# An MLP's second token half, prepared in pieces between six opening pairs on VectorE

## The chip, the cores and the metric

The kernel runs on one core of a Trainium2 chip. A core has a matrix engine (TensorE, PE in the profile), three engines for elementwise work (VectorE or DVE, ScalarE or ACT, GpSimd or POOL), a queue that issues transfers (SyncE or SP), an on-chip memory of 128 partitions that the kernel divides into tiles, and an accumulator memory (PSUM) into which TensorE writes. The metric is the time of one execution in device microseconds; lower is better.

## The reference

A small encoder of two layers over 1024 tokens of width 1024. Layer 0 mixes tokens with windowed attention beside a pooling mixer, layer 1 with latent attention beside a recurrent block. Each layer ends with the same kind of MLP, and this is what the change touches:

```python
def rmsnorm(x, g):
    y = x * lax.rsqrt(jnp.mean(x * x, axis=-1, keepdims=True) + EPS)
    return y * g

def sq_relu_mlp(h, w1, w2):
    u = jax.nn.relu(h @ w1)        # 1024 x 1024 times 1024 x 4096
    return (u * u) @ w2            # 1024 x 4096 times 4096 x 1024

for layer in range(2):
    x = x + mixer(layer, rmsnorm(x, norm[layer]))
    x = x + sq_relu_mlp(rmsnorm(x, norm_mlp[layer]), w_mlp1[layer], w_mlp2[layer])
return rmsnorm(x, final_norm)
```

All of it is in 32-bit floats.

## The kernel before

**Layout.** The activations stand transposed: channels on the partitions, tokens along the free axis. X is eight tiles of 128 channels by 1024 tokens. A token half is 512 columns; `lo` and `hi` in the norm of the MLP are the first and the second half.

**Split operands.** TensorE gets each 32-bit operand as two parts, high and low: ScalarE rounds the value to the matrix format (the high part, `rnd`, line 122, or line 278 with a sign), VectorE subtracts to get the low part (`sub`, line 130, or line 279). Each 128-deep step is three matmuls: high by high, low by high, high by low. `block()` (line 272) makes such a pair for a 128x512 operand; blocks of activations are named `hb`, blocks of weights `wb`.

**Strassen-like products.** An MLP's first matrix product works on 2x2 blocks: two token halves, two channel halves, two weight chunks (a pair p out of 16). Seven products serve for eight. For the weights the seven operands are A11, A12, A22 and sums S1 to S4, which POOL adds; for the activations they are B11 and B21 (the first token half's two channel halves) and t2, t3, T1, t4, B22, each of four channel chunks, which need the second token half also. One product (line 367) is 4 chunks times 3 matmuls, 12 matmuls of 128x512.

**Order in an MLP (`mlp`, line 348).** NS = 4 pairs open the MLP. For these, only the two products that need the first token half are done first: `head` (A11 by B11, copied to t1) and `head2` (A12 by B21, then relu and square to u11). After them `rest` does the five other products of each of these pairs, with their weights loaded again, and then pairs 4 to 15 run with all seven products. The results u11, u12, u21, u22 and their sums go to DRAM (`put`, line 378). The second matrix product (`second`, line 470) reads them back, in three groups of pairs, and adds into X, which `load_x` (line 247) reads back from DRAM before it begins. The last two pairs (TAIL) are plain products.

**Weights as a stream.** `w_stream` yields one weight block after the other in a given order, and `Ahead` keeps three more than the one that is taken (W_AHEAD = 3). So the instructions that make a block stand in the program four products ahead of its use. A block sits in one of eight weight tiles (W_BUFS); four of the eight hold two prefetched weights of TAIL all through an MLP.

**The norm of the MLP (`SNorm`, line 1453).** `part(c, cut)` is called by the output projection before the MLP when channel chunk c of a token half is final. It squares the chunk on ScalarE and adds it to `acc` on POOL (`square_add`, line 238); in the second half it writes X to DRAM (line 1472). `sums` (a matmul with ones, line 220, and the root) and `finish` (the factor broadcast by matmul, line 231, and copied to RB) follow. `finish(0)` scales all eight chunks of the first half into new tiles H (line 1492) and makes B11 and B21. `finish(1)`, which is called after the second head, does the whole second half: it scales eight chunks, subtracts (lines 1507 and 1509, VectorE), subtracts and adds on POOL (lines 1512 and 1516), and makes the 20 blocks t2, t3, T1, t4, B22.

**The projection before it.** In the even layer `outproj_halves` (line 730) does eight output chunks for the first token half, then eight for the second, and loads each of its four weights for both halves. In the odd layer, the loop at line 1143 does the same with eight weights.

**Buffers.** Most tiles of 128x1024 come from one pool with 41 buffers (G_BUFS). U and H2 hand out halves of such a tile.

**What sets the order.** The program is traced in Python; a planner then orders the instructions of each engine, with the traced order as their priority, by a simulated timeline, and adds the waits. On the chip each engine and each queue runs its list in that order.

The wait for a tile of the pool is one of these waits, and so a transfer into a tile that isn't free yet holds up what stands behind it in the queue.

Of the kernel before, what the change touches and what calls it, by code (L numbers as in the profile page):

```python
# [15 lines left out]
P = 128  # L16
# [30 lines left out]
class Trunk:  # L47
# [89 lines left out]
    def requests(self, ph):  # L137
        a = self.a
        if ph == "even":
            r = [(a["e_w_in"][i], S) for i in (4, 5, 0, 1, 2, 3)] + [(a["e_w_pool"], N2)]  # L140
            r += [(a["e_w_in"][i], S) for i in (9, 8, 7, 6)]
            r += [(a["e_w_out"][1][m], S, "act", "pool") for m in range(4)]
            return r + [(a["e_w_out"][0][m], S) for m in range(4)] * 2
# [203 lines left out]

    def mlp(self, l, nb, nxt, dram):
# [4 lines left out]
        main = ("A11", "S2", "S3", "S1", "A12", "A22", "S4")  # L353
        start = range(NS)
        order = [x for p in start for x in [(p, "A11")] + [(p - 1, "A12")] * (p > 0)] + [(NS - 1, "A12")]
        order += [(NP + p, b) for p in start for b in ("S2", "S3", "S1", "A22", "S4")]
        order += [(p, b) for p in range(NS, NP) for b in main]
        stream = Ahead(self.w_stream(l, order, False), W_AHEAD)
# [71 lines left out]
        for p in start:  # L430
            ps = self.PS("q")
            early[p] = (*head(p, ps), ps)
            if p == 0:
                nb.sums(1)
            if p == 1:
                nb.finish(1)
            if p:
                head2(p - 1, early[p - 1][2], early[p - 1][1])
        head2(NS - 1, early[NS - 1][2], early[NS - 1][1])
        k = 0  # L440
# [24 lines left out]
        X = self.load_x(nb.spill)  # L465
# [13 lines left out]

        for g, pairs in enumerate(GROUPS):  # L480
# [7 lines left out]
            B = self.banks(1 - k)  # L488
            second(B, pairs, True, False)
            for m in range(4):  # L490
                V.tensor_tensor(X[4 + m][:, h1], B[m], X[4 + m][:, h1], op=ALU.add)  # L491
            second(A, pairs, False, True)
# [237 lines left out]
    def outproj_halves(self, X, Yh, Yl, done):  # L730

        for n in range(2):
            s = slice(n * N2, (n + 1) * N2)
            for mm in range(NC // 2):
                W = self.weight()
                for j in range(2):
                    m = 2 * mm + j
                    ps = self.PS("op")
                    self.mm3(ps, [(W[0][:, (j * 4 + k) * P:(j * 4 + k + 1) * P],
                                   W[1][:, (j * 4 + k) * P:(j * 4 + k + 1) * P], Yh[k][:, s], Yl[k][:, s])  # L740
                                  for k in range(4)])
                    self.nc.vector.tensor_tensor(X[m][:, s], ps, X[m][:, s], op=ALU.add)
                    done(m, HALVES[n])
# [709 lines left out]
class SNorm:  # L1453

    cuts = [(0, N2), (N2, S)]

    def __init__(self, t, X, gname, spill):
        self.t, self.X, self.g, self.spill = t, X, gname, spill  # L1460
        self.acc, self.r, self.T = {}, {}, {}
        self.RB = t.G("RB")
        self.H = None

    def part(self, c, cut):
        t = self.t
        n = HALVES.index(cut)
        if c == 0:
            self.acc[n] = t.tp.tile([P, N2], F32, tag="acc", name=t.nm("acc"), bufs=2)
        t.square_add(self.acc[n], self.X[c][:, slice(*cut)], c == 0)  # L1470
        if n == 1:
            t.nc.sync.dma_start(self.spill[c * P:(c + 1) * P, :], self.X[c])
            if c == 2:
                self.sums(0)
            if c == 4:
                self.finish(0)
# [4 lines left out]
    def finish(self, n):  # L1481
        t, nc = self.t, self.t.nc
        V = nc.vector
        s = slice(n * N2, (n + 1) * N2)
        lo, hi = slice(0, N2), slice(N2, S)
        t.rb_bcast(self.r[n], self.RB[:, s])
        if n == 0:
            self.H = [t.G("H") for _ in range(NC)]
        H = self.H

        def scaled(c):
            V.scalar_tensor_tensor(H[c][:, s], self.X[c][:, s], t.col(self.g, c), self.RB[:, s],
                                   op0=ALU.mult, op1=ALU.mult)

        def blocks(name, xs, neg=False):
            self.T[name] = [t.block("hb", x, neg=neg) for x in xs]

        if n == 0:
            for name, r in (("B11", range(4)), ("B21", range(4, 8))):
                for c in r:  # L1500
                    scaled(c)
                blocks(name, [H[c][:, s] for c in r])
            return
        t2 = [t.U("t2") for _ in range(4)]
        for c in range(4):
            scaled(c)
# [12 lines left out]


class Ahead:
# [5 lines left out]
    def take(self):  # L1527
        while len(self.have) <= self.ahead:
# [3 lines left out]
            self.have.append(x)  # L1532
        return self.have.pop(0)
# [88 lines left out]
NS = 4  # L1622
# [16 lines left out]
def trunk(tc, a, phases=("even", "mlp0", "odd", "mlp1", "final")):  # L1639
    PSUM = bass.MemoryType.PSUM  # L1640
    with tc.tile_pool(name="cst", bufs=1) as cst, tc.tile_pool(name="sm", bufs=4) as sm, \
# [11 lines left out]
        def follow(i):  # L1653

            def make(X):
# [3 lines left out]
                    SNorm(t, X, gains[ph], xm[int(ph[-1])])  # L1659
# [104 lines left out]
```

## Time and profile before

| | us |
|---|---|
| median of 3 runs | 2253.13 (2248.68 to 2254.84) |
| the profiled execution | 2256.08 |
| its span | 2254.2 |
| TensorE busy in it | 2067.0 |
| VectorE busy | 1539.7 |
| ScalarE busy | 1063.9 |
| GpSimd busy | 865.4 |
| matmuls of the first MLP products, L367 (2688) | 643.7 |
| matmuls of the second MLP products, L477 (2352) | 540.4 |

The profile has one page for an execution, and views that can be asked for: the same stretch of time by engine (windows), groups of instructions by line, the waits, and the timeline. Busy time of TensorE includes pipelining: at full rate, matmuls of 128x512 start every 0.225 us though each shows as about 0.39 us. "Idle before, releaser" names what ended an engine's wait. The granted clock is the share of full speed that TensorE was given.

MLP 0 begins at about 313 us and MLP 1 at about 1542 us in the profiled execution. Their second stages begin at 701.6 and 1916.5 us.

### The profile page before, as it was taken

What the parts mean: (1) busy time and instruction counts of PE and PEld (TensorE: products, weight loads), DVE (VectorE), ACT (ScalarE), POOL (GpSimd) and SP (SyncE); (2) the same over time, 40 slices, a digit from 0 to 9 for tenths busy, and PEclk for the clock granted to TensorE, in tenths of its full rate; (3) what the DMA queues carried; (4) which work ended last, traced back from release to release, by engine and by line L of the source; (5) the groups of instructions that cost most, each with busy time, mean ns of one, the idle gap of its engine ahead of it and who ended that gap; (6) DMA issues with size and microseconds to landing.
All of it is one profiled execution on the core that took longest, in us unless ns stands there. A gap on an engine that the chain in (4) does not pass through costs nothing. (4 is left out here: it accounts for less than half of the span.)

```text
span 2254.2 us, 27294 instructions
## 1 busy us (share of the span) xinstructions
PE 2067.0 (92%) x9600; PEld 1695.6 (75%) x9600; DVE 1539.7 (68%) x2345; ACT 1063.9 (47%) x1857; POOL 865.4 (38%) x659
## 2 busy tenths in 40 slices
PE   7989984999998999999997999896799998999997
PEld 5867763777776788888775998785577776788887
DVE  7788756655555877764897888617665564877874
ACT  5247543444444444331565777634444444444423
POOL 4143244322224241332557675464322221513314
PEclk9999986999999999999999999998899999999999
DMA  5630041444357536122102000233253445554412
GB/s 168 159 113 20 22 157 61 164 145 149 108 171 290 185 102 195 66 80 89 33 33 56 10 15 6 94 126 126 104 180 119 149 146 212 197 193 133 148 37 75
DMA packets 113240, 261.32 MB, mean 116 GB/s; under 512 B 19408, under 2 KB 21584, under 8 KB 113104
## 3 DMA queue, kind: packets, MB, share of 16 engines
q1 hardware_dynamic: 113104, 259.59, 34.5%
q8 instruction: 75, 1.23, 0.2%
q14 instruction: 61, 0.50, 0.1%
HBM read 178.28 MB, written 72.35 MB: 111 GB/s over the span
## 5 line engine op out<-in xcount | busy, mean ns | idle before, releaser
L367 PE MATMUL q<-hb,wb 128*128 128x512 f32 x2688 | 643.7, 399 | 104.4 <-ACT wb L122 76.0
L367 PEld LDWEIGHTS q<-hb,wb 128*128 128x128 f32 x2688 | 511.0, 192 | 235.5 <-ACT wb L122 88.1
L477 PE MATMUL q<-ub,wb 128*128 128x512 f32 x2352 | 540.4, 392 | 15.5 <-ACT ub L122 10.5
L477 PEld LDWEIGHTS q<-ub,wb 128*128 128x128 f32 x2352 | 443.8, 189 | 112.2 <-ACT ub L122 11.3
L130 DVE TENSOR_TENSOR wb<-raw,wb 128x512 fp32r<-128x512 f32 x268 | 226.0, 850 | 130.5 <-ACT wb L122 129.8
L122 ACT CAST wb<-raw 128x512 fp32r<-128x512 f32 x268 | 163.3, 618 | 201.2 <-PE q L367 107.8
L327 POOL TENSOR_TENSOR sum<-raw 128x512 f32<-128x512 f32 x32 | 41.7, 1302 | 404.8 <-DMA raw<-in_w_dram 306.6
L130 DVE TENSOR_TENSOR ub<-ut,ub 128x512 fp32r<-128x512 f32 x168 | 136.2, 821 | 57.9 <-ACT ub L122 57.8
L122 ACT CAST ub<-ut 128x512 fp32r<-128x512 f32 x168 | 101.5, 619 | 149.7 <-DMA ut<-ut_12t 19.0
L130 DVE TENSOR_TENSOR wb<-sum,wb 128x512 fp32r<-128x512 f32 x152 | 128.3, 846 | 58.0 <-ACT wb L122 57.4
L245 POOL TENSOR_TENSOR acc<-acc,sq 128x512 f32<-128x512 f32 (+1 forms) x70 | 101.9, 1458 | 138.2 <-ACT sq L244 136.5
L122 ACT CAST wb<-sum 128x512 fp32r<-128x512 f32 x152 | 93.5, 618 | 120.7 <-PE q L367 50.8
L185 PE MATMUL z<-Hh,wh 128*128 128x512 f32 x336 | 132.6, 398 | 9.6 <-ACT wh L122 9.6
L185 PE MATMUL z<-Hl,wh 128*128 128x512 f32 x336 | 133.2, 397 | 4.0 <-DVE Hl L1439 3.8
L185 PE MATMUL z<-Hh,wl 128*128 128x512 f32 x336 | 132.0, 394 | 0.0
L323 POOL TENSOR_TENSOR sum<-raw,raw 128x512 f32<-128x512 f32 x28 | 40.1, 1435 | 221.7 <-DMA raw<-in_w_dram 156.0
L122 ACT CAST wh<-raw 128x1024 fp32r<-128x1024 f32 (+1 forms) x53 | 54.0, 1018 | 114.3 <-PE z L185 38.9
L1092 PE MATMUL cav<-cpT,VS 128*128 128x256 f32 x512 | 102.2, 303 | 5.4 <-ACT cpT L1321 2.8
L1302 PE MATMUL ms<-Kt,Qt 128*128 128x512 f32 (+1 forms) x384 | 100.5, 398 | 2.3 <-ACT e L1309 1.4
L1322 DVE TENSOR_TENSOR cpT<-ctp,cpT 128x512 fp32r<-128x512 f32 x128 | 86.6, 686 | 16.6 <-ACT cpT L1321 13.9
L185 PE MATMUL op<-yh,wh 128*128 128x512 f32 x244 | 96.6, 397 | 1.2 <-DVE ya L855 0.6
L1074 POOL TENSOR_SCALAR e<-e,csm 128x1024 f32<-128x1024 f32 x64 | 71.9, 1126 | 64.6 <-DVE csm L1073 51.4
(349 smaller groups left out, 3874.3 us busy)
## 6 DMA issues: line engine op xcount, KB each, us to landing
raw<-in_w_dram SPq DMA_DIRECT2D x136, 512.0 KB, 4.6
xm<-X SPq DMA_DIRECT2D x16, 512.0 KB, 3.0
X<-xm SPq DMA_DIRECT2D x16, 512.0 KB, 5.6
raw<-in_o_w_out_dram SPq DMA_DIRECT2D x16, 512.0 KB, 3.4
raw<-in_e_w_out_dram SPq DMA_DIRECT2D x12, 512.0 KB, 3.5
raw<-in_o_w_in_dram SPq DMA_DIRECT2D x11, 512.0 KB, 3.4
raw<-in_e_w_in_dram SPq DMA_DIRECT2D x10, 512.0 KB, 4.4
X<-in_x_dram SPq DMA_DIRECT2D x16, 256.0 KB, 5.4
```

Of the source, the lines that this page charges most:

```text
L122: self.nc.scalar.copy(out, x)
L130: e.tensor_tensor(out, x, y, op=ALU.subtract)
L185: self.nc.tensor.matmul(ps, l, r, start=(first and i == 0), stop=(last and i == n - 1))
L245: (eng or nc.gpsimd).tensor_tensor(acc, acc, sq, op=ALU.add)
L323: add(x, blk(p, 1, 0), blk(p, 1, 1), op=ALU.add)
L327: add(s1, blk(p, 1, 0), blk(p, 1, 1), op=ALU.add)
L367: nc.tensor.matmul(ps, a, b, start=(first and c == 0 and i == 0), stop=(c == 3 and i == 2), skip_group_check=True)
L477: nc.tensor.matmul(ps[m], a, b, start=(first and j == 0 and i == 0), stop=(j == len(pairs) - 1 and i == 2), skip_group_check=True)
L1074: nc.gpsimd.tensor_scalar(e, e, sm, 1.0, op0=ALU.mult, op1=ALU.mult)
L1092: nc.tensor.matmul(ACC[0][:, (p % 2) * 256:(p % 2 + 1) * 256], VS[h][:, kb * P:(kb + 1) * P], pp[:, t * N2 + ii * 256:t * N2 + (ii + 1) * ...
L1302: nc.tensor.matmul(ps[:, s], l[rows, qs], r[rows, s], start=(i == 0), stop=(i == 2))
L1322: nc.vector.tensor_tensor(pp[:, N2:], tp, pp[:, :N2], op=ALU.subtract)
```

## The change

- `NS` goes from 4 to 6: six pairs open an MLP instead of four.
- `SNorm` makes the weight stream itself when it is created. In the second half of the projection, `part` calls `sums(0)` at chunk 1, the factor at chunk 2, makes the first four weight blocks (`fill`) at chunk 4, and from chunk 3 on scales the first half and makes B11 and B21, a few chunks at each call.
- X is scaled in place; there are no tiles H. X is written to DRAM by token halves, as each is final.
- From chunk 4 of the second half on, the sum of squares is added on VectorE instead of POOL.
- `finish(1)` becomes the generator `late`, in ten pieces. Two pieces are traced per opening pair, one before and one after `head2`. Its subtractions and additions are all on VectorE.
- `mlp` reads X back later: chunks 4 to 7 ahead of the second product group's use of them, chunks 0 to 3 after it.
- `outproj_halves` keeps its four weights for both halves, and loads each once.

```diff
-            return r + [(a["e_w_out"][0][m], S) for m in range(4)] * 2
+            return r + [(a["e_w_out"][0][m], S) for m in range(4)]
...
             early[p] = (*head(p, ps), ps)
             if p == 0:
                 nb.sums(1)
-            if p == 1:
-                nb.finish(1)
-            if p:
+                late = nb.late()
+            else:
+                next(late)
                 head2(p - 1, early[p - 1][2], early[p - 1][1])
+                next(late)
         head2(NS - 1, early[NS - 1][2], early[NS - 1][1])
+        for _ in late:
+            pass
...
-        X = self.load_x(nb.spill)
+        X = [self.G("X") for _ in range(NC)]
...
+        def load(ms):
+            for m in ms:
+                dma(X[m], nb.spill[m * P:(m + 1) * P, :])
...
             B = self.banks(1 - k)
+            if g == 0:
+                load(range(4, 8))
             second(B, pairs, True, False)
...
+            if g == 0:
+                load(range(4))
             second(A, pairs, False, True)
...
             for mm in range(NC // 2):
-                W = self.weight()
+                if n == 0:
+                    ws.append(self.weight())
+                W = ws[mm]
...
+        self.stream = t.first_stream(l)
...
-        t.square_add(self.acc[n], self.X[c][:, slice(*cut)], c == 0)
-        if n == 1:
-            t.nc.sync.dma_start(self.spill[c * P:(c + 1) * P, :], self.X[c])
-            if c == 2:
-                self.sums(0)
-            if c == 4:
-                self.finish(0)
+        t.square_add(self.acc[n], self.X[c][:, s], c == 0, t.nc.vector if n and c > 3 else None)
+        t.nc.sync.dma_start(self.spill[c * P:(c + 1) * P, s], self.X[c][:, s])
+        if n == 0:
+            return
+        if c == 1:
+            self.sums(0)
+        elif c == 2:
+            self.factor(0)
+        elif c >= 3:
+            if c == 4:
+                self.stream.fill()
+            for k in ((0, 1), (2, 3), (4,), (5,), (6, 7))[c - 3]:
+                self.scaled(k, 0)
+                self.T["B11" if k < 4 else "B21"].append(t.block("hb", self.X[k][:, :N2]))
...
+    def scaled(self, c, n):
+        s = slice(n * N2, (n + 1) * N2)
+        x = self.X[c][:, s]
+        self.t.nc.vector.scalar_tensor_tensor(x, x, self.t.col(self.g, c), self.RB[:, s], op0=ALU.mult, op1=ALU.mult)
+
+    def late(self):
+        t, H, T = self.t, self.X, self.T
+        V = t.nc.vector
         lo, hi = slice(0, N2), slice(N2, S)
+        for name in ("t2", "t3", "T1", "t4", "B22"):
+            T[name] = []
+        self.factor(1)
+        t2 = []
         for c in range(4):
-            scaled(c)
+            self.scaled(c, 1)
             V.tensor_tensor(H[c][:, lo], H[c][:, hi], H[c][:, lo], op=ALU.subtract)
-            scaled(4 + c)
+            self.scaled(4 + c, 1)
+            t2.append(t.U("t2"))
             V.tensor_tensor(t2[c], H[c][:, lo], H[4 + c][:, hi], op=ALU.subtract)
-        blocks("t2", t2)
+            T["t2"].append(t.block("hb", t2[c]))
+            yield
         for c in range(4):
-            nc.gpsimd.tensor_tensor(H[c][:, hi], H[c][:, hi], H[4 + c][:, hi], op=ALU.subtract)
-        blocks("t3", [H[c][:, hi] for c in range(4)])
-        blocks("T1", [H[c][:, lo] for c in range(4)])
+            V.tensor_tensor(H[c][:, hi], H[c][:, hi], H[4 + c][:, hi], op=ALU.subtract)
+            T["t3"].append(t.block("hb", H[c][:, hi]))
+            if c % 2:
+                yield
         for c in range(4):
-            nc.gpsimd.tensor_tensor(H[4 + c][:, lo], H[4 + c][:, lo], t2[c], op=ALU.add)
-        blocks("t4", [H[4 + c][:, lo] for c in range(4)])
-        blocks("B22", [H[4 + c][:, hi] for c in range(4)], neg=True)
+            T["T1"].append(t.block("hb", H[c][:, lo]))
+        yield
+        for c in range(4):
+            V.tensor_tensor(H[4 + c][:, lo], H[4 + c][:, lo], t2[c], op=ALU.add)
+            T["t4"].append(t.block("hb", H[4 + c][:, lo]))
+            if c % 2:
+                yield
+        for c in range(4):
+            T["B22"].append(t.block("hb", H[4 + c][:, hi], neg=True))
+        yield
...
-NS = 4
+NS = 6
```

`first_stream` gives the order of the weight blocks that `mlp` gave itself before: A11 of pair 0, then A11 of pair p and A12 of pair p - 1 in turn, A12 of the last opening pair, the five blocks of each rest pair, and the seven of each other pair.

More of the change, by code (lines that the diff above doesn't have):

```diff
@@ L346, in w_stream, with first_stream @@
             yield prep(p, b)
+    def first_stream(self, l):
+        start = range(NS)
+        order = [x for p in start for x in [(p, "A11")] + [(p - 1, "A12")] * (p > 0)] + [(NS - 1, "A12")]
+        order += [(NF // 2 + p, b) for p in start for b in ("S2", "S3", "S1", "A22", "S4")]
+        order += [(p, b) for p in range(NS, NF // 2) for b in ("A11", "S2", "S3", "S1", "A12", "A22", "S4")]
+        return Ahead(self.w_stream(l, order, False), W_AHEAD)
     def mlp(self, l, nb, nxt, dram):
@@ L352, in mlp @@
         NP = NF // 2
-        main = ("A11", "S2", "S3", "S1", "A12", "A22", "S4")
         start = range(NS)
[L355 to L358, printed above, removed]
+        stream = nb.stream
         def product(ps, blocks, first, last):
@@ L730, in outproj_halves @@
     def outproj_halves(self, X, Yh, Yl, done):
+        ws = []
         for n in range(2):
@@ L1457, with __init__ @@
     cuts = [(0, N2), (N2, S)]
-    def __init__(self, t, X, gname, spill):
+    def __init__(self, t, X, gname, spill, l):
         self.t, self.X, self.g, self.spill = t, X, gname, spill
-        self.acc, self.r, self.T = {}, {}, {}
+        self.acc, self.r, self.T = {}, {}, {"B11": [], "B21": []}
         self.RB = t.G("RB")
-        self.H = None
+        self.stream = t.first_stream(l)
     def part(self, c, cut):
@@ L1467, in part @@
         n = HALVES.index(cut)
+        s = slice(*cut)
         if c == 0:
             self.acc[n] = t.tp.tile([P, N2], F32, tag="acc", name=t.nm("acc"), bufs=2)
-        t.square_add(self.acc[n], self.X[c][:, slice(*cut)], c == 0)
-        if n == 1:
-            t.nc.sync.dma_start(self.spill[c * P:(c + 1) * P, :], self.X[c])
-            if c == 2:
-                self.sums(0)
+        t.square_add(self.acc[n], self.X[c][:, s], c == 0, t.nc.vector if n and c > 3 else None)
+        t.nc.sync.dma_start(self.spill[c * P:(c + 1) * P, s], self.X[c][:, s])
@@ L1475, in part, with factor @@
+        if n == 0:
[5 more added lines that the diff above has]
+        elif c >= 3:
             if c == 4:
-                self.finish(0)
+                self.stream.fill()
+            for k in ((0, 1), (2, 3), (4,), (5,), (6, 7))[c - 3]:
+                self.scaled(k, 0)
+                self.T["B11" if k < 4 else "B21"].append(t.block("hb", self.X[k][:, :N2]))
     def sums(self, n):
         self.r[n] = self.t.rb_sum(self.acc[n], D)
-    def finish(self, n):
-        t, nc = self.t, self.t.nc
-        V = nc.vector
+    def factor(self, n):
+        self.t.rb_bcast(self.r[n], self.RB[:, n * N2:(n + 1) * N2])
@@ L1484, in finish @@
+    def scaled(self, c, n):
         s = slice(n * N2, (n + 1) * N2)
-        lo, hi = slice(0, N2), slice(N2, S)
[L1486 to L1496, printed above, removed]
@@ L1498, in finish @@
-        if n == 0:
-            for name, r in (("B11", range(4)), ("B21", range(4, 8))):
-                for c in r:
-                    scaled(c)
-                blocks(name, [H[c][:, s] for c in r])
-            return
-        t2 = [t.U("t2") for _ in range(4)]
+        x = self.X[c][:, s]
[3 more added lines that the diff above has]
+        V = t.nc.vector
+        lo, hi = slice(0, N2), slice(N2, S)
+        for name in ("t2", "t3", "T1", "t4", "B22"):
+            T[name] = []
+        self.factor(1)
+        t2 = []
@@ L1505, in finish @@
         for c in range(4):
-            scaled(c)
+            self.scaled(c, 1)
             V.tensor_tensor(H[c][:, lo], H[c][:, hi], H[c][:, lo], op=ALU.subtract)
-            scaled(4 + c)
+            self.scaled(4 + c, 1)
+            t2.append(t.U("t2"))
             V.tensor_tensor(t2[c], H[c][:, lo], H[4 + c][:, hi], op=ALU.subtract)
-        blocks("t2", t2)
+            T["t2"].append(t.block("hb", t2[c]))
+            yield
         for c in range(4):
-            nc.gpsimd.tensor_tensor(H[c][:, hi], H[c][:, hi], H[4 + c][:, hi], op=ALU.subtract)
@@ L1525, in __init__, with fill @@
         self.gen, self.ahead, self.have = gen, ahead, []
-    def take(self):
+    def fill(self):
         while len(self.have) <= self.ahead:
@@ L1532, in take @@
             self.have.append(x)
+    def take(self):
+        self.fill()
         return self.have.pop(0)
@@ L1658, in make @@
                     Norm(t, X, gains[ph], xs if ph == "odd" else None) if ph in ("even", "odd") else \
-                    SNorm(t, X, gains[ph], xm[int(ph[-1])])
+                    SNorm(t, X, gains[ph], xm[int(ph[-1])], int(ph[-1]))
                 return box[i]
```

## The prediction

> **What bounds the kernel now.** I read the page first, for the engine that bounds each stage.
>
> ```profile
> span 2254.2 us, 27294 instructions
> ...
> PE 2067.0 (92%) x9600; PEld 1695.6 (75%) x9600; DVE 1539.7 (68%) x2345; ACT 1063.9 (47%) x1857; POOL 865.4 (38%) x659
> ...
> PE   7989984999998999999997999896799998999997
> ...
> PEclk9999986999999999999999999998899999999999
> ```
>
> TensorE (PE) is the bound nearly everywhere: most slices are 9. Two places stand out: slices 5 to 7, and 27 and 28 counted from 1. There the TensorE row falls to 4 to 8, the granted clock with it. These are the openings of the two MLPs. The windows view sets the two openings beside the pairs that follow and a stretch without holes:
>
> ```profile
> 313.00:384.00 71.00, 31.45 (x109) 23.59 (x109) 49.11 (x68) 27.52 (x49) 33.03 (x15) 0.66 0.18 67
> 1542.20:1600.00 57.80, 25.21 (x107) 19.62 (x106) 43.99 (x58) 23.08 (x42) 29.38 (x15) 0.73 0.19 68
> 384.00:440.00 56.00, 52.76 (x227) 41.91 (x226) 31.31 (x46) 23.59 (x41) 15.51 (x12) 1.00 0.44 160
> 910.00:960.00 50.00, 50.00 (x222) 41.41 (x221) 36.06 (x46) 16.85 (x26) 10.00 (x7) 1.00 0.19 64
> ```
>
> Columns: stretch, its length, busy time and count of PE, weight loads, VectorE (DVE), ScalarE (ACT), GpSimd (POOL), then clock, DMA share, GB/s. The last row is my ruler: 222 matmuls in 50 us, 0.225 us each; a product (12 matmuls) is 2.70 us. The next view groups the same two openings by line, one answer for each:
>
> ```profile
> L367 PE MATMUL q<-hb,wb 128*128 128x512 f32 x92 | 29.9, 488 | 38.5 <-ACT wb L122 33.4 <-DVE wb L130 4.8 <-ACT RB L235 0.2
> L220 PE MATMUL ss<-ones,acc 128*128 128x1 f32 x8 | 1.1, 253 | 1.0 <-POOL acc L245 1.0
> ...
> L367 PE MATMUL q<-hb,wb 128*128 128x512 f32 x90 | 24.0, 421 | 32.6 <-ACT wb L122 25.7 <-DVE wb L130 6.2 <-ACT RB L235 0.7
> ```
>
> Opening of MLP 0: 92 x 0.225 = 20.7 us, and two groups of eight small norm matmuls (sum and broadcast) at 1.1 us; 71 - 22.9 = **48 us lost**. Of MLP 1: 90 x 0.225 + 2.2 = 22.5; 57.8 - 22.5 = **35 us lost**. 38.5 and 32.6 us of this are idle, the rest slow clock. Why PE idles is in the timeline, PE first, then DVE, then the DMA queue (SPq):
>
> ```profile
> 320.83 5.98 PE L367 MATMUL q<-hb,wb 128*128 128x512 f32 x14 [7.65 <-ACT wb L122]
> ...
> 339.47 3.01 PE L367 MATMUL q<-hb,wb 128*128 128x512 f32 x12 [0.20 <-ACT RB L235]
> 368.21 1.22 PE L367 MATMUL q<-hb,wb 128*128 128x512 f32 x2 [25.73 <-ACT wb L122]
> 374.26 11.05 PE L367 MATMUL q<-hb,wb 128*128 128x512 f32 x35 [4.83 <-DVE wb L130]
> ```
> ```profile
> 339.45 5.39 DVE L1492 SCALAR_TENSOR_TENSOR H<-X,cols,RB 128x512 f32<-128x512 f32 x8 [9.12 <-ACT RB L235]
> ...
> 349.57 2.48 DVE L130 TENSOR_TENSOR hb<-t,hb 128x512 fp32r<-128x512 f32 x4
> 353.86 15.20 DVE L130 TENSOR_TENSOR hb<-H,hb 128x512 fp32r<-128x512 f32 x12 [1.80 <-ACT hb L122]
> 368.98 4.62 DVE L279 SCALAR_TENSOR_TENSOR hb<-H,hb 128x512 fp32r<-128x512 f32 x4
> 373.52 1.88 DVE L130 TENSOR_TENSOR wb<-raw,wb 128x512 fp32r<-128x512 f32 x3
> ```
> ```profile
> 313.85 1.79 SPq L304 DMA_DIRECT2D raw<-in_w_dram  x3
> ```
>
> The second half's preparation runs as one block, 339.45 to 373.52 = 34 us, and the weight blocks of the last opening pairs come behind it on DVE and ACT. PE has five products of work, then stands 25.7 us. MLP 1 shows the same gap. MLP 0 also loses 7.65 us at its start: its first raw weights are only issued at 313.85, when the output projection has ended.
>
> **The change part by part.** *1. The late block, in pieces.* Alone, a tensor_tensor or a low-part split takes 2.48/4 = 0.62 us, a scaling 5.39/8 = 0.67. Beside POOL a split takes 15.20/12 = 1.27. On DVE alone the block is 8 scalings (5.4), 8 subtractions and 8 more operations that now run half on POOL (16 x 0.62 = 9.9), 16 splits (9.9) and 4 negated splits. Those I see only beside POOL or ScalarE waits, 4.62/4 = 1.16; alone they lie between the scaling's 0.67 and 1.16 and I take 0.67, its own kind of instruction (2.7, at most 4.6). Sum **27.9 us** (to 29.8) for 34. It is cut into ten pieces of 2.5 to 3.2 us, one per product.
>
> Beside a piece go one weight split (0.62) and 2.70 us of PE work. So DVE needs 3.1 to 3.8 us where PE needs 2.70: DVE falls behind by some 0.7 us a product, 7 us in ten. But a weight block is made four products ahead (W_AHEAD), a cover of 4 x 2.70 = 10.8 us, and blocks t2, t3, T1, t4, B22 are first needed in this order after the opening, B22 four products into the first rest pair. The opening lasts 12 x 2.70 + 2.2 = 34.6 us instead of 8 products: two more opening pairs bring 4 products as cover, without adding any in all, and each reloads one raw tile (0.5 MB).
>
> *2. The first half's blocks and the first weights, earlier.* They move into the projection's second half. MLP 0: from the third of eight groups on, about 13 us of PE, DVE gets 5 evictions, 4 sums that POOL had, 8 scalings, 8 splits and 4 weight splits:
>
> ```profile
> L742 DVE TENSOR_TENSOR X<-op,X x15: 673/691/693, 277.3 to 312.8; 128x512 f32<-128x512 f32 x15
> ...
> L245 POOL TENSOR_TENSOR acc<-acc,sq x70: 725/1295/5686, 12.4 to 2227.1; 128x512 f32<-128x512 f32 x63, 128x256 f32<-128x256 f32 x7
> ```
>
> 5 x 0.69 + 4 x 0.62 + 5.4 + 12 x 0.62 = 18.8 us in about 13: DVE is some 6 us late at the projection's end. The first head needs B11 alone, which comes first; B21 is wanted two products (5.4 us) later. So the 7.65 us go, and late() starts some 9 us after the end: an estimate, 6 of backlog and 3 for sum, root and broadcast, which wait their turn on DVE (it can't be later than today's 339.45, 26 us after the projection's end). 27.9 + 8 weight splits (5.0) + small operations (2) put its end at 44 us; B22's use is at 34.6 + 4 x 2.70 = 45.4. It just fits. MLP 1's projection has groups twice as long, so DVE is at rest there.
>
> I leave 9 us lost in MLP 0's opening and 8 in MLP 1's: about 4 for weight splits behind a piece, 4 for PE's sum and broadcast, which wait on DVE's backlog. The ends are 0 and the 26 each of rival A. Gain: 48 - 9 + 35 - 8 = **66 us**.
>
> The clock matters for any stall that stays (the windows view again, after the gap).
>
> ```profile
> 370.00:380.00 10.00, 5.74 (x14) 4.49 (x15) 6.00 (x7) 1.69 (x3) 3.64 (x3) 0.50 0.00 1
> 380.00:390.00 10.00, 10.00 (x45) 8.28 (x44) 4.12 (x6) 2.92 (x6) 0.00 (x0) 0.99 0.22 76
> ```
>
> After the gap the clock stays at 0.50 for 5.74 us of matmuls: 2.9 us lost on top of a long gap, none after the short ones I forecast. The Trainium skill, "TensorE: Matmul & The Clock Gate", section Part 1, has the clock come back after about 3.4 us of sustained work; by that, an estimate, 1.7 us would be lost. The trace is longer and decides.
>
> *3. X in place, spilled by halves.* 16 spills of 256 KB for 8 of 512 on the queue; the late scaling waits for the second half's spill. Eight H tiles fall away. That matters, since the 41 buffers are all held today (first row: the DMA queue's waits; second: the page's DMA issues, median from issue to landing):
>
> ```profile
> SPq L304 <- DVE hb L130: 37.4, 2, 18.7
> ```
> ```profile
> raw<-in_w_dram SPq DMA_DIRECT2D x136, 512.0 KB, 4.6
> ```
>
> Twice, 37.4 us in all, a raw load stood until a block's split gave back a buffer. I count this in term 1. The spills lie beside the projection's last groups, 0; without that cover the late scaling waits for one landing per MLP, at most the 4.6 us of a raw tile twice its size.
>
> *4. Output weights kept* (MLP 0): four loads, casts and splits fewer, beside PE's sixteen groups (their evictions L742 run to 312.8 in the row above); PE hides them today and nothing comes of it, 0. Were the cover not whole, it would be a gain of some us.
>
> *5. X read back later.* Now eight loads stand ahead of the second stage's first raws:
>
> ```profile
> 672.87 9.91 SPq L251 DMA_DIRECT2D X<-xm  x8
> 682.83 2.16 SPq L304 DMA_DIRECT2D raw<-in_w_dram  x4
> ```
> ```profile
> 701.59 38.64 PE L477 MATMUL q<-ub,wb 128*128 128x512 f32 x163 [4.69 <-ACT ub L122]
> ...
> 1916.48 24.46 PE L477 MATMUL q<-ub,wb 128*128 128x512 f32 x100 [5.78 <-ACT ub L122]
> ```
>
> The gaps are 4.69 and 5.78 us, 10.5 in all. The releaser is a cast on ACT, which also has the last pair's relu to do, so the loads need not be all of it: I take 5, between 0 and 10.5. The later loads have five products (13.5 us) to land in; if late, a few us are given back (bound -6).
>
> Sum: 66 + 5 - 1 (two more rest pairs for main ones) = 70. The profiled execution took 2256.1 us (span 2254.2); 2256.1 - 70 = 2186. The median of the runs is 2253.1, 3 below it, so between 2183 and 2186; since the residuals are likelier larger than smaller, I say **2186** for the median.
>
> **The rivals.** *A, the block stays a block.* The instruction order is made by a planner; today DVE ran all 8 scalings ahead of the first subtraction though they are traced in turn. If it puts the pieces together again ahead of the weights, the block ends 9 + 27.9 us after the projection, PE has worked 13.5 + 2 of it: 22 us idle and some 4 of slow clock, 26 lost per MLP. Gain 22 + 9 + 5 = 36: **2217**. For it: that order. Against: the weight splits are now traced between pieces, and across instructions traced far apart (weights behind the block) the order of before follows the trace. This is also the case in which the change does not do what it says.
>
> *B, slower: buffers.* After the opening 28 blocks, 6 tiles of early results, 2 raws, 1 sum and 3 results are held, 40 of 41, against 38 today. A raw pair for the next rest pair then waits for the last one's release. Its price is the landing (4.6 us), two POOL sums, cast and split:
>
> ```profile
> L327 POOL TENSOR_TENSOR sum<-raw 128x512 f32<-128x512 f32 x3 | 3.9, 1290 | 34.1 <-DMA raw<-in_w_dram 25.1 <-issue 9.0
> ```
>
> 4.6 + 2 x 1.29 + 2 x 0.62 = 8.4 us; bare in all 12 rest pairs that is 101, 31 more than the gain: **2284**. It decides from 70/12 = 5.8 us a pair. Against: four products (10.8 us) lie between request and use, and each pair done frees a tile; four rest pairs today lose 3.24 us of 56 together. The Trainium skill, "Perfetto Trace Analysis", section Optimization Strategy, says that the same gap repeating on the engine that should be full can mean that there is no room for the next tile; today's rest pairs show such gaps only of that small size.
>
> *C, better:* residuals near 0 and both transitions closed: 48 + 35 + 10 = 93, **2160**.
>
> **How the numbers follow.** Forecast 0.66 (2165 to 2206), A 0.22 (2206 to 2228), C 0.05, B 0.05, no gain 0.02. About 0.3%, 7 us, is what a measurement of this kernel can tell from no change. Range **2165 to 2222**: the forecast and most of A; left out are C, B, no gain and A's tail. Faster 0.93, within 0.02, slower 0.05.
>
> **What would show it.** Each step right: no PE gap over 5 us between projection and first rest pair, clock 1.0 there, DVE full for some 45 us with weight splits between pieces, POOL without work on H, no 7.65 us gap. Step 5: raws ahead of X loads, gaps under 3 us. Wrong: weight splits behind all pieces (A), or gaps of 6 us on raw loads in each rest pair (B).

## The result, and the profile after

The changed kernel takes 2197.53 us (median; 2195.6 to 2201.01), the kernel before 2251.24 us beside it (2248.68 to 2254.84): ratio 0.9762, interval 0.9742 to 0.9782. That is 53.7 us faster, where 70 were forecast and 2186 us named; 2197.5 lies in the range. The two profiled executions differ by more, 2254.2 - 2193.8 = 60.4 us of span, since the one before (2256.08 us) took longer than any of its timed runs and the one after (2195.6) as little as the shortest of its own.

The page of the changed kernel: span, busy times, and the rows of TensorE and its clock.

```profile
span 2193.8 us, 27305 instructions
...
PE 2060.6 (94%) x9600; PEld 1687.3 (77%) x9600; DVE 1536.4 (70%) x2365; ACT 1056.5 (48%) x1853; POOL 812.4 (37%) x635
...
PE   7999998999999999999997999898999999999997
...
PEclk9999998999999999999999999999999999999998
```

In the two openings one 8 each is left, slice 7 in MLP 0 and slice 28 in MLP 1. The windows view of the changed kernel gives the openings by the prediction's ruler:

```profile
313.00:384.00 71.00, 58.60 (x233) 45.93 (x232) 53.23 (x84) 37.07 (x69) 14.25 (x9) 0.86 0.25 89
1507.60:1560.00 52.40, 40.09 (x171) 31.91 (x170) 42.09 (x67) 29.49 (x54) 6.65 (x4) 0.87 0.28 101
```

233 matmuls less the 16 small ones, at 0.225, plus 2.2, are 51.0 of 71 us: **20 us lost** where 48 were. 155 x 0.225 + 2.2 = 37.1 of 52.4: **15 lost** where 35 were. So the openings gave 48 of the 66 us forecast. The clock is 0.86 and 0.87 there, not 1.0. TensorE is idle for 71.00 - 58.60 = 12.4 us of the first stretch; the other 7.6 us are busy time over the ruler, most of it at the slow clock. In MLP 1 it is 12.3 and 3.0 us. Where the idle time is, the timeline of the changed kernel shows: TensorE in MLP 0 and, in the last two of its rows, in MLP 1, then VectorE, ScalarE and the DMA queue in MLP 0:

```profile
315.39 10.67 PE L371 MATMUL q<-hb,wb 128*128 128x512 f32 x46
325.90 0.95 PE L220 MATMUL ss<-ones,acc 128*128 128x1 f32 x8
328.43 1.43 PE L231 MATMUL q<-ident,rr 128*128 128x128 f32 x8 [1.59 <-DVE rr L211]
330.54 5.49 PE L371 MATMUL q<-hb,wb 128*128 128x512 f32 x12 [0.67 <-ACT RB L235]
342.44 1.22 PE L371 MATMUL q<-hb,wb 128*128 128x512 f32 x2 [6.41 <-ACT wb L122]
346.20 26.12 PE L371 MATMUL q<-hb,wb 128*128 128x512 f32 x106 [2.55 <-DVE wb L130]
...
1532.46 1.22 PE L371 MATMUL q<-hb,wb 128*128 128x512 f32 x2 [8.28 <-ACT wb L122]
1536.83 13.52 PE L371 MATMUL q<-hb,wb 128*128 128x512 f32 x50 [3.15 <-DVE wb L130]
...
330.52 5.39 DVE L1514 SCALAR_TENSOR_TENSOR X<-X,cols,RB 128x512 f32<-128x512 f32 x8 [2.24 <-ACT RB L235]
...
345.46 1.29 DVE L130 TENSOR_TENSOR wb<-raw,wb 128x512 fp32r<-128x512 f32 x2
...
363.86 2.49 DVE L279 SCALAR_TENSOR_TENSOR hb<-X,hb 128x512 fp32r<-128x512 f32 x4
...
341.76 1.14 ACT L122 CAST wb<-raw 128x512 fp32r<-128x512 f32 x2 [0.50 <-DMA raw<-in_w_dram]
...
302.81 1.35 SPq L304 DMA_DIRECT2D raw<-in_w_dram  x3
...
337.35 0.32 SPq L382 DMA_DIRECT2D ut_1B<-t  x1
337.76 8.62 SPq L304 DMA_DIRECT2D raw<-in_w_dram  x5
```

The gap of 25.73 us is now two, 6.41 and 2.55 us. Both are in the sixth product, as before (2 matmuls on their own stood ahead of the first row: 2 + 46 + 12 are five products): its first matmul waits for the cast of its weight block, its third for the block's split. The expectations below call it the seventh. The 7.65 us at the start are gone. VectorE still runs all eight scalings in a row and 16 more operations before the next weight split, at 345.46. And the queue issues the raw weights of pairs 3 to 5 only at 337.76, behind a write-back of pair 1. That left three suspects for the loss: **R**, raw tiles late in the queue; **L**, the late part starting 15 us after the projection; **D**, the planner's order on VectorE.

### The profile page after: what moved, and what is told of

The parts are those of the page before. It is cut to its first block, busy times and chain, and to the rows that moved or that the text cites. A ratio compares the mean times of both kernels' runs of the same rounds, so it can differ in the third digit from the quotient of the medians.

```text
span 2193.8 us, 27305 instructions
## 1 busy us (share of the span) xinstructions
PE 2060.6 (94%) x9600; PEld 1687.3 (77%) x9600; DVE 1536.4 (70%) x2365; ACT 1056.5 (48%) x1853; POOL 812.4 (37%) x635
## 5 line engine op out<-in xcount | busy, mean ns | idle before, releaser
L371 PE MATMUL q<-hb,wb 128*128 128x512 f32 x2688 | 637.9, 396 | 60.8 <-ACT wb L122 28.4
L371 PEld LDWEIGHTS q<-hb,wb 128*128 128x128 f32 x2688 | 504.9, 190 | 192.8 <-ACT wb L122 44.8
L245 POOL TENSOR_TENSOR acc<-acc,sq 128x512 f32<-128x512 f32 (+1 forms) x62 | 84.4, 1364 | 126.4 <-ACT sq L244 124.5
L185 PE MATMUL op<-yl,wh 128*128 128x512 f32 x252 | 98.8, 393 | 0.0
L185 PE MATMUL op<-yh,wl 128*128 128x512 f32 x252 | 97.9, 393 | 0.0
```

Of the source, the lines that this page charges most:

```text
L185: self.nc.tensor.matmul(ps, l, r, start=(first and i == 0), stop=(last and i == n - 1))
L245: (eng or nc.gpsimd).tensor_tensor(acc, acc, sq, op=ALU.add)
L371: nc.tensor.matmul(ps, a, b, start=(first and c == 0 and i == 0), stop=(c == 3 and i == 2), skip_group_check=True)
```

## The experiments

All times are medians, each with its ratio to the kernel before on the same chip; "the changed kernel" is 2197.5, ratio 0.9762. The runs were on several chips, where the kernel before took 2250.0 to 2253.1 us, and the intervals of the ratios are 6 to 9 us wide: a difference of 3 us says little.

### 1. First raw tiles of all six pairs asked for at once

```diff
+        for p in early:
+            raw(p, 0)
         for p, b in order:
             yield prep(p, b)
```

Here `early` holds the six opening pairs; the loop runs when the stream is first filled.

> The first raw tiles of all six opening pairs are asked for when the stream is first filled, ahead of the write-back of u11 of pairs 0 and 1; everything else as in the changed kernel (2197.5 us; some 23 us lost in MLP 0's opening and 15.5 in MLP 1's). Theory R (raw tiles of pairs 3 to 5 stand on SP's queue behind a write that waits for pair 1's second product, so the seventh weight block comes late): the gaps of 6.41 and 8.28 us before the seventh product go and the 2.55 and 3.15 behind them shrink: 12 to 20 us faster, 2178 to 2186. Theory D (the planner puts DVE's pieces together ahead of the weight splits, so an earlier raw tile helps nothing): less than 4 us. Theory L (the late part starts 13.5 to 15 us after the projection, not 9): the gaps move to the first products on t2; 4 to 10 us faster at most.

2186.05 us, 0.9702 (0.9688 to 0.9715): 11.5 us faster than the changed kernel. That is just short of R's lower bound and over L's and D's. Its timeline, TensorE and then ScalarE (L373 is the product, L371 before):

```profile
332.35 3.01 PE L373 MATMUL q<-hb,wb 128*128 128x512 f32 x12 [0.68 <-ACT RB L235]
336.56 0.73 PE L373 MATMUL q<-hb,wb 128*128 128x512 f32 x2 [1.19 <-ACT wb L122]
340.18 7.87 PE L373 MATMUL q<-hb,wb 128*128 128x512 f32 x22 [2.89 <-DVE wb L130]
...
330.87 0.62 ACT L122 CAST wb<-raw 128x512 fp32r<-128x512 f32 x1 [2.40 <-PE q L373]
...
341.37 0.62 ACT L122 CAST hb<-t 128x512 fp32r<-128x512 f32 x1 [4.33 <-DVE t L1531]
```

The sixth product now has its block in time, and the gaps, at the seventh, are 1.19 and 2.89. But two things have changed at once: the tiles come earlier, and the weight casts now stand ahead of the first cast of t2 on ScalarE. Run 9 takes them apart.

### 2. The place of the sum and the broadcast

```diff
-            early[p] = (*head(p, ps), ps)
+            early[p] = (*head(p, ps, p == 1), ps)
...
-            product(ps, nb.T["B21"], False, True)
+            product(ps, nb.T["B21"], False, True, p == 0)
...
+                    if pin and c == 0 and i == 0:
+                        self.pin(m)
```

The first matmul of pair 1's `head` is held behind the sum's matmuls, that of pair 0's `head2` behind the broadcast's.

> Only the place of two groups of small norm matmuls on PE is fixed: the sum directly behind the first product, the broadcast behind two more, by holding the first matmul of the next product behind each. In the changed kernel the sum came after three products and the broadcast after four. Theory L (late start): the eight scalings begin 3 to 5 us earlier after the projection and 6 to 10 us go in the two openings, 2187 to 2191. Theories R and D: the raw tiles and the order on DVE are unchanged, so the seventh weight block comes as much earlier as the block of scalings only if DVE sets it; with R 0 to 3 us, since the raw tile is still issued behind the write-back; a new wait on the accumulator or on the factor may cost up to 3.

2200.67, 0.9768 (0.9755 to 0.9781): no gain, so L is not borne out in this form. TensorE's and VectorE's rows of MLP 0 and TensorE's of MLP 1, from its timeline:

```profile
325.54 1.87 PE L220 MATMUL ss<-ones,acc 128*128 128x1 f32 x8 [5.54 <-DVE acc L245]
...
337.24 5.39 DVE L1516 SCALAR_TENSOR_TENSOR X<-X,cols,RB 128x512 f32<-128x512 f32 x8 [8.39 <-ACT RB L235]
...
1539.34 1.22 PE L371 MATMUL q<-hb,wb 128*128 128x512 f32 x2 [6.49 <-ACT wb L122]
```

In MLP 0 the fixed place cost time itself: TensorE stood 5.54 us ahead of the sum, and the broadcast waited behind two more products, so the scalings even came later (337.24). In MLP 1 the gap fell from 8.28 to 6.49 us, too little to make up for it. An earlier start that doesn't make TensorE wait wasn't tried.

### 3, 4 and 7. One block, four pairs, and both

```diff
-                next(late)
+                if p == 1:
+                    for _ in late:
+                        pass
                 head2(p - 1, early[p - 1][2], early[p - 1][1])
-                next(late)
...
-NS = 6
+NS = 4
```

Run 3 has the first part of this, run 4 the second, run 7 both.

> All pieces of the second half's preparation are traced in one go between the first product of pair 1 and the second product of pair 0; six opening pairs, VectorE alone and all else as in the changed kernel. If the pieces do what the forecast said (rival A at 2217 when they are put together again): 15 to 26 us slower than the changed kernel, 2212 to 2224. Theory D (the planner has put them together already): within 4 us of 2197.5. Half and half: about 8 us slower.

> Four opening pairs in place of six, all else as in the changed kernel. If the two more opening pairs bring cover as forecast (4 products, 10.8 us, in each MLP; end of the late part 42 us after the projection against B22's use at 8 x 2.70 + 2.2 + 10.8 = 34.6): 8 to 10 us more lost in each opening, 2212 to 2218. If the openings are set by the seventh weight block alone, which comes at the same time either way: within 4 us of 2197.5. One raw reload fewer per pair is worth nothing beside PE.

> Both undone: four opening pairs, and the late part traced in one go; the rest (first half's blocks and first weights earlier, sums and late part on VectorE alone, X in place and read back later, output weights kept) as in the changed kernel. One go alone measured 2222.4, four pairs alone 2212.9, that is 24.9 and 15.4 over 2197.5. If the two add up: 2238, and the other parts of the change are worth some 15 us against 2252.9. If they are one gain (cover against one block; with one block the two more pairs bring nothing): 2223 to 2228, and the other parts are worth 25 to 30. If the pieces pay only with six pairs: 2213 to 2218.

One block: 2222.42, 0.9863 (0.985 to 0.9877), 24.9 us slower than the changed kernel. Four pairs: 2212.87, 0.9817 (0.9803 to 0.9832), 15.3 slower. Both: 2225.56, 0.9886 (0.9872 to 0.9899), 28.0 slower, not 40. So for the most part it is one gain. With the late part in one block two more pairs bring 3 us, hardly more than nothing; in pieces they bring 15. The timeline of the kernel with one block and six pairs shows that D, in the sense that the planner had put the pieces together already, falls:

```profile
356.72 2.26 PE L371 MATMUL q<-hb,wb 128*128 128x512 f32 x4 [19.35 <-ACT wb L122]
...
1561.97 2.26 PE L371 MATMUL q<-hb,wb 128*128 128x512 f32 x4 [21.41 <-ACT wb L122]
```

These are the 22 us of rival A, 19.35 and 21.41 measured. That its 2217 was only 5 short of this kernel is in part luck: it counted 5 us for the later loads of X, which run 5 puts at 15.7.

### 5. X read back ahead of the second stage

```diff
-        X = [self.G("X") for _ in range(NC)]
+        X = self.load_x(nb.spill)
...
-            if g == 0:
-                load(range(4, 8))
...
-            if g == 0:
-                load(range(4))
```

> X is read back by eight loads ahead of the second stage, as before the change; all else as in the changed kernel (2197.5 us). The forecast gave the later loads 5 us, between 0 and 10.5: 2198 to 2208, most likely 2203, with gaps of some 5 us ahead of each second stage's first matmul. If the later loads give back as much as they take (gaps of 2.36 us at 690.0 and 2.05 us at 1881.8 in the changed kernel, behind a weight cast on ACT): 2200 to 2204. If the gaps came from ACT's relu work in the last pair and not from the loads: within 2 us of 2197.5.

2213.25, 0.983 (0.9817 to 0.9844): the later loads are worth **15.7 us**, outside all three expectations. The timeline of this kernel at the end of MLP 0's first stage, TensorE and queue:

```profile
662.82 2.97 PE L371 MATMUL q<-hb,wb 128*128 128x512 f32 x12 [0.88 <-DVE u L405]
666.67 2.96 PE L371 MATMUL q<-hb,wb 128*128 128x512 f32 x12 [0.88 <-DVE u L412]
674.32 2.07 PE L484 MATMUL q<-ub,wb 128*128 128x512 f32 x4 [4.69 <-ACT ub L122]
...
648.47 8.53 SPq L251 DMA_DIRECT2D X<-xm  x8
657.22 4.00 SPq L304 DMA_DIRECT2D raw<-in_w_dram  x4
```

And of the changed kernel:

```profile
660.20 2.97 PE L371 MATMUL q<-hb,wb 128*128 128x512 f32 x12 [0.88 <-DVE u L405]
663.00 3.79 PE L484 MATMUL q<-ub,wb 128*128 128x512 f32 x16
666.63 2.88 PE L371 MATMUL q<-hb,wb 128*128 128x512 f32 x12
...
690.01 4.61 PE L484 MATMUL q<-ub,wb 128*128 128x512 f32 x12 [2.36 <-ACT wb L122]
...
645.84 6.40 SPq L304 DMA_DIRECT2D raw<-in_w_dram  x4
```

The raw tiles go out at 645.84 in place of 657.22, some 9 us earlier, since run 5 is 2.6 us behind by then. Not only is the 4.69 gap gone. The second stage's first 16 matmuls now stand ahead of the last pair's last product, so 4.69 us and one of the two waits of 0.88 go, and 2.36 come back at 690.01.

The whole stretch, from the last pair's wait for `t` to the first matmul behind the second stage, takes 290.85 us in MLP 0 here (656.26 to 947.11) and 286.35 in the changed kernel (653.64 to 939.99); in MLP 1 it takes 294.18 and 285.37. These 13.3 us are most of the 17.9 by which the two profiled executions differ. Between the kernel before (288.14 and 294.26) and the changed kernel it is 10.7 us.

### 6. GpSimd does t3 and t4 again

```diff
-            V.tensor_tensor(H[c][:, hi], H[c][:, hi], H[4 + c][:, hi], op=ALU.subtract)
+            t.nc.gpsimd.tensor_tensor(H[c][:, hi], H[c][:, hi], H[4 + c][:, hi], op=ALU.subtract)
...
-            V.tensor_tensor(H[4 + c][:, lo], H[4 + c][:, lo], t2[c], op=ALU.add)
+            t.nc.gpsimd.tensor_tensor(H[4 + c][:, lo], H[4 + c][:, lo], t2[c], op=ALU.add)
```

> The eight tensor_tensor operations for t3 and t4 run on GpSimd again, as before the change; pieces, six pairs and all else as in the changed kernel. The forecast priced them on VectorE alone at 8 x 0.62 = 5.0 us of its time and the splits beside GpSimd at 1.27 in place of 0.62 us. If this matters: the late part ends 2 to 6 us later and 4 to 12 us are lost in both openings together, 2201 to 2210. If the seventh weight block's raw tile alone sets the openings (theory R): within 3 us. If VectorE is the bound and the eight operations are all taken off it at no cost: 4 to 8 us faster, 2190 to 2194.

2205.42, 0.9799 (0.9786 to 0.9813): 7.9 us slower, in the range given for the case that VectorE alone matters. Its timeline on VectorE:

```profile
352.87 5.82 DVE L130 TENSOR_TENSOR hb<-X,hb 128x512 fp32r<-128x512 f32 x4 [3.46 <-ACT hb L122]
358.61 3.45 DVE L130 TENSOR_TENSOR wb<-raw,wb 128x512 fp32r<-128x512 f32 x2
```

Beside GpSimd the four splits take 1.46 us each, and VectorE waits 3.46 us ahead of them. The Trainium skill, "SBUF — State Buffer", section "Who interferes with whom", says that a VectorE instruction with two inputs in that memory contends with a GpSimd instruction that reads it, and that what they share is an exclusive lock; the trace agrees: 0.62 us alone, 1.46 here.

### 8. Weight blocks five products ahead

```diff
-W_AHEAD = 3
+W_AHEAD = 4
```

This is on the kernel of run 1.

> Two things on the changed kernel: the six first raw tiles asked for at once (measured alone 2186.1 us, ratio to before 0.9702) and weight blocks made five products ahead in place of four. If cover between a block's request and its use still sets the gaps that are left (some 7 to 12 us in each opening, 0.9 us of waits on weight splits and casts in each of 12 rest pairs): 6 to 20 us under 2186. If VectorE and ScalarE are behind and not the requests: within 4 us of 2186. If buffers run short (rival B): over 2192.

2211.43, 0.9826 (0.9809 to 0.9842): 25 us slower than run 1. The DMA queue now waits for the late part's last blocks, which in run 1 it does not (what for: us in total, times, longest):

```profile
SPq L304 <- DVE hb L279: 40.6, 2, 21.0
```

A raw tile asked for one product earlier finds no free buffer until the late part's last splits (L279) give one back, and the queue stands for up to 21 us. That is how rival B begins. But the time is not lost there. From the first product of MLP 0 to its first main pair (a pair with all seven products) run 8 takes 144.8 us and run 1 144.9, and in MLP 1 142.7 and 144.2. From there to the last pair's wait for `t` run 8 takes 207.1 and 209.0 us, run 1 194.4 and 193.7. The same place in the main pairs of MLP 0, run 8 first:

```profile
518.82 6.91 PE L373 MATMUL q<-hb,wb 128*128 128x512 f32 x22 [1.78 <-DVE wb L130]
...
519.67 39.82 PE L373 MATMUL q<-hb,wb 128*128 128x512 f32 x166 [0.27 <-ACT t L391]
```

TensorE waits for the split of a weight block, and the 22 matmuls behind it take 6.91 us where 22 x 0.225 are 5.0. This comes back every second pair, and no raw tile waits for a buffer there (480 to 620 us). Why these splits come late isn't shown.

### 9. Write-backs issued by ScalarE

```diff
-            dma(d, x)
+            (nc.scalar.dma_start if k[0] == "B" else dma)(d, x)
```

This is on the changed kernel.

> On the changed kernel, the write-backs of results that end in a relu (u11, u22, u21, u12: 64 of them) are issued by ScalarE, which makes them, in place of SP; raw tiles are asked for where they were. Theory R (SP's queue is in order and its raw tiles wait behind write-backs that wait for their data): the raw tiles of pairs 3 to 5 go out in time and the gaps of 6.41 and 8.28 us go, as in the run with the first raw tiles ahead of the write-backs: 2180 to 2188; if the queue's waits also make the weight waits of the rest pairs (some 17 us in each MLP), 2160 to 2180. If the raw tiles were late because they were asked for late and not because of the queue: within 4 us of 2197.5. If raw tiles that come earlier take the buffers that others need, as may be behind the 25 us lost with weight blocks five products ahead (2211.4 against 2186.1): 2200 to 2225.

2214.28, 0.9837 (0.9818 to 0.9856): 17 us slower, so R as a matter of the queue falls. From its timeline, queue, ScalarE, then TensorE:

```profile
317.48 1.35 SPq L304 DMA_DIRECT2D raw<-in_w_dram  x3
...
338.33 0.62 ACT L122 CAST hb<-t 128x512 fp32r<-128x512 f32 x1 [0.59 <-DVE t L1529]
338.86 0.58 ACT L389 COPY t<-q 128x512 f32<-128x512 f32 x1
339.33 1.14 ACT L122 CAST wb<-raw 128x512 fp32r<-128x512 f32 x2
...
340.01 1.22 PE L371 MATMUL q<-hb,wb 128*128 128x512 f32 x2 [8.25 <-ACT wb L122]
344.38 29.61 PE L371 MATMUL q<-hb,wb 128*128 128x512 f32 x118 [3.15 <-DVE wb L130]
```

The three raw tiles are issued at 317.48, 20 us earlier than in the changed kernel, and the gaps are as long as ever. The cast of the sixth block has its place on ScalarE behind the first casts of t2, and these wait for VectorE's scalings and subtractions. What held the block is **the written order of ScalarE and VectorE**, not the queue. In the changed kernel, too, ScalarE waited only 0.50 us for the tile itself (the row at 341.76). Run 1 gained because asking earlier also moved the weights' casts and splits ahead of the late part in that order. Most of the 17 us are lost in the main pairs: from the first of them to the last pair's wait for `t` TensorE takes 199.9 and 200.9 us in the two MLPs, 192.9 and 193.7 in the changed kernel. The queue's waits for the sums that it writes back (L382 <- DVE T L423) grew from 142.8 to 431.9 us in all; that they cost these 14 us isn't shown.

### 10. The pieces held apart on VectorE

```diff
-            self.scaled(c, 1)
+            t.behind(self.scaled(c, 1), prev)
```

`prev` is the split of the piece before the last one. The same goes for `scaled(4 + c, 1)` and the arithmetic of t3 and t4, on the kernel of run 1.

> The first raw tiles asked for at once (2186.1 us), and the pieces of the late part kept apart on VectorE: each piece's first operations are held behind the low-part split of the piece before the last one, so that not all eight scalings run first; the weight splits are left free. Theory D (what is left in the openings, some 12 us in MLP 0 and 10 in MLP 1, comes from the planner running scalings, t3 and t4 arithmetic ahead of the splits that the next product needs): 4 to 12 us faster, 2174 to 2182. If VectorE's total work between the projection and the first rest pair sets it, in whatever order: within 3 us of 2186. If holding pieces back makes VectorE wait for ScalarE's casts: 2 to 8 us slower.

2194.09, 0.9741 (0.9724 to 0.9758): 8 us slower than run 1, about what the third expectation gave. TensorE's timeline in MLP 0:

```profile
336.73 5.30 PE L380 MATMUL q<-hb,wb 128*128 128x512 f32 x22 [0.24 <-DVE wb L136]
347.02 13.79 PE L380 MATMUL q<-hb,wb 128*128 128x512 f32 x48 [4.99 <-ACT t L398]
```

The wait for the weight split did fall, from 2.89 to 0.24 us, as D would have it. A new gap of 4.99 us takes more: it ends with ScalarE's copy of a product's result (L398), which stands behind casts of t2 that wait for VectorE. So holding the pieces apart in this way costs more than it brings, and whether another order would bring D's gain is open.

### 11. The stream not filled early

```diff
-            if c == 4:
-                self.stream.fill()
```

> On the changed kernel, the weight stream is not filled ahead of the MLP's first product; the first raw tiles are asked for when the first product is traced, as before the change; the first half's blocks stay in the projection's second half. The forecast counted the gap of 7.65 us at MLP 0's start and nothing at MLP 1's: 7 to 11 us slower with the slow clock behind the gap, 2204 to 2209. If the planner asks for the tiles early anyway: within 3 us of 2197.5. If both MLPs lose the landing of a raw tile (4.5 us), two sums' worth of cast and split and the first cover of four blocks: 15 to 25 us slower.

2199.59, 0.977 (0.9751 to 0.9789): the same. The queue's row in its timeline:

```profile
303.87 1.35 SPq L304 DMA_DIRECT2D raw<-in_w_dram  x3
```

The planner sends the tiles out 10 us earlier than before the change (313.85) without the early fill. The 7.65 us went by another part: the first half's blocks in the projection, the half-size spills or the buffers that H no longer takes. These weren't tried alone.

### 12. The second half's sums on GpSimd again

```diff
-        t.square_add(self.acc[n], self.X[c][:, s], c == 0, t.nc.vector if n and c > 3 else None)
+        t.square_add(self.acc[n], self.X[c][:, s], c == 0)
```

This is on the kernel of run 1.

> The first raw tiles asked for at once (2186.1 us), and the four sums of squares of the second half that the change put on VectorE are on GpSimd again in each MLP. If VectorE's backlog at the projection's end (the forecast's 6 us, with these four sums, 4 x 0.62) makes the late part start late: it starts some 2 us earlier in MLP 0, and 2 to 6 us go in both, 2180 to 2184. If the sum waits for the chain of sums and GpSimd's 1.29 us a step makes that chain longer: 2 to 6 us slower. If the place of the sum on TensorE sets the start: within 2 us.

2185.07, 0.9717 (0.9702 to 0.9731): the same as run 1. The four sums on VectorE neither cost nor bring anything that shows.

## Why the prediction was right, and where its size was off

- **The bound and the main mechanism held.** The late block behind which the weights stood was the main loss; pieces with more pairs took 28.0 us of it away (run 7), half of the 53.7 in all. With the 15.7 us of run 5 some 10 are left, if the two add, for all other parts of the change; of these only runs 6, 11 and 12 tried some.
- **The late part's length was right, in part by luck.** Forecast 27.9 + 5.0 + 2 = 35 us; in the changed kernel it runs from 330.52 to 366.35, 35.8 us. In it six splits beside GpSimd's first sums took 7.01 us, 1.17 each in place of 0.62, and in turn none of the small operations and one weight split fewer fell into it. **Its start was not right:** 15 us after the projection's end in MLP 0, not 9. Runs 2 and 12, which aimed at the start, gained nothing, so an earlier start by itself is not shown to be worth anything.
- **The step that failed is the residual of term 1: "I leave 9 us lost in MLP 0's opening and 8 in MLP 1's: about 4 for weight splits behind a piece".** It was 20 and 15. I counted a weight block's cover from the traced order, four products, and let one split slip in beside each piece. In the order that the planner wrote, the sixth block's split stands behind eight scalings and 16 operations, and its cast behind two casts of t2: 6.41 + 2.55 us in MLP 0 and 8.28 + 3.15 in MLP 1 in place of 4 each. Run 1 put them ahead and got 11.5 us back; run 9 showed that the tiles' arrival was not it. The 4 us for the sum and the broadcast were enough: the waits around them are 1.59 + 0.67 us in MLP 0.
- **The clock was put at nothing there** ("none after the short ones I forecast"), and this is the other half of what the residual lacked: 7.6 us of busy time over the ruler in MLP 0 and 3.0 in MLP 1. By the same sum it was 8.6 and 2.8 before the change, which hardly touched it.
- **Rival A was a matter of degree.** The planner put together part of the late block (the scalings and most of the subtractions and additions), not all: 9 us of gap in MLP 0, where run 3 has one of 19.35.
- **Step 5 was sized too small: 5 us, at most 10.5; measured 15.7 (run 5).** I bounded it by the two gaps ahead of the second stage's first matmul. In the profiled executions 13.3 us of it are in the stretch from the last pair to the second stage's end, and 10.7 between the kernel before and the changed one. The eight loads also held the raw tiles back by some 9 us, and with these in time the second stage's first matmuls are done within the last pair. The bound should have taken in the last pair's waits, and the clock behind the gap.
- **Step 2's first half was right in effect, not in cause.** The 7.65 us went, but not by the early fill (run 11).
- **VectorE alone:** worth 7.9 us (run 6); the forecast had it within term 1.
- **Rival B** wasn't met by this change. With one more block of cover the queue does stand for a buffer (run 8), but the 25 us of that run are lost elsewhere.
- **Of the signs named**, no 7.65 us gap, GpSimd without work on H and gaps under 3 us at the second stage came. No gap over 5 us (6.41 and 8.28) and a clock of 1.0 (0.86 and 0.87) did not.

So the openings gave 18 us less than forecast and the transitions, between the two profiled executions, 6 more: 70 - 18 + 6 = 58, near their 60.4. The rest of the way to 53.7 is that this pair lies apart by more than the medians. That the error of the forecast is no larger than 16 us is in part luck, since the two went opposite ways. The best version is run 1: 2186.05 us, 0.9702 to before, 11.5 us under the changed kernel.

## What to carry to other kernels

Cover counted in the traced order is worth only what the written order of each engine leaves of it: read how many instructions stand ahead of the one that the bound waits for, on every engine it passes, before pricing a residual. A request that is made earlier can pay by moving its followers in that order even where its data was not what came late, and more cover isn't always better: one block more cost 25 us, and not at the place where the queue stood for a buffer. When loads are moved behind others, count what the others gain and not only the gap that stands in the trace. And price the slow clock for every opening that keeps a gap.

## What the runs showed of the hardware

The clock was low after gaps much shorter than those I had feared. The windows view of the changed kernel:

```profile
312.00:315.40 3.40, 3.40 (x10) 2.61 (x9) 3.40 (x7) 0.20 (x1) 0.00 (x0) 0.51 0.34 125
326.00:331.00 5.00, 2.74 (x18) 2.39 (x17) 1.47 (x7) 0.79 (x2) 0.00 (x0) 0.81 0.13 49
331.00:336.10 5.10, 5.03 (x12) 3.34 (x11) 5.10 (x9) 0.04 (x1) 0.00 (x0) 0.52 0.00 0
```

After two waits of 1.59 and 0.67 us around sixteen small matmuls, twelve matmuls run at 0.52 and take 5.1 us in place of 2.7. At 312 the same happens after two waits of 0.92 us. In run 1 nearly the same stretch, after waits of 0.91 and 0.92, is at full clock:

```profile
312.00:316.00 4.00, 3.73 (x15) 2.74 (x15) 4.00 (x8) 2.30 (x5) 1.22 (x1) 1.00 0.90 356
```

So in these two traces a stretch with little work in it cost up to 2.4 us more without any long gap, and whether it did varied. The Trainium skill, "TensorE: Matmul & The Clock Gate", section "HAM oscillation — how this bites in real kernels", gives idle gaps over about 3.4 us as what to avoid; by that rule alone neither place would have slowed down, and here the measurement decides.
